# Eight single PSUM banks, a later fetch of x, and seven-product pairs at other places in a decoder layer

## The chip, the core and the metric

The kernel runs on one core of a Trainium2 chip. The metric is the device time of one execution in microseconds (us). The engines are TensorE (PE: matmuls; PEld: its weight loads), VectorE (DVE), ScalarE (ACT), GpSimd (POOL) and SyncE (SP, which here only starts DMAs). Each has its own queue, which it works through in order; semaphores hold an instruction back until what it needs is done. All matmul results land in PSUM, which has eight banks of 512 float32 columns on each of 128 partitions.

## The reference: what is computed

One layer of a decoder on x, 256 tokens by 2048 channels, in float32: a feed-forward half step, a mixer of two kinds of attention, a second feed-forward half step. Each is set between two RMS norms.

```python
for l in range(DEPTH):          # DEPTH = 1
    h = rmsnorm(x, ffn1_pre_g[l])
    x = x + 0.5 * rmsnorm(swiglu_ffn(h, ffn1_w_in[l], ffn1_w_out[l]), ffn1_post_g[l])
    h = rmsnorm(x, mix_pre_g[l])
    y = hybrid_mixer(h, w_in[l], ..., w_branch_sb[l], w_branch_nsa[l], w_out[l])
    x = x + rmsnorm(y, mix_post_g[l])
    h = rmsnorm(x, ffn2_pre_g[l])
    x = x + 0.5 * rmsnorm(swiglu_ffn(h, ffn2_w_in[l], ffn2_w_out[l]), ffn2_post_g[l])

def swiglu_ffn(h, w_in, w_out):
    gate, up = jnp.split(h @ w_in, 2, axis=-1)      # w_in 2048 x 11264
    return (jax.nn.silu(gate) * up) @ w_out         # w_out 5632 x 2048
```

The mixer projects h to queries, keys, values and gates, runs eight heads of stick-breaking attention and eight heads of native sparse attention (compressed, selected and window keys), projects both branches, merges them by gates and projects once more (w_out, 2048 x 2048).

## The kernel before

**Numbers in two parts.** Every float32 factor is written as hi + lo, two values of a shorter format that PE multiplies at full rate, and a product is three matmuls: hi by hi, lo by hi, hi by lo. For a weight, ACT writes hi (`cast`, L1106) into the ring whi, and DVE writes lo = w - hi (`low`, L1109) into wlo. PE's own matmuls all stand in one line, L1322.

**Steps, units, pairs, items.** The layer is a sequence of steps, each a product of the 256 rows with up to 1024 columns of a weight matrix. A step's destination is two banks for the upper 128 rows (h = 0) and two for the lower (h = 1). A *unit* is 128 rows of weights (one kt) by 1024 columns; for one half h it is an *item* of six matmuls, 2 banks by 3 terms. A *pair* is two neighbouring units, 1 MB, and comes by one DMA. In the two feed-forward networks some pairs are computed as a 2x2 block product with seven products in place of eight: three items of 9, 6 and 6 matmuls for four of 6, so 21 matmuls for 24. Such a pair needs sums and differences of weight blocks (DVE, L1189 and L1175) and of the left factors (`side_sums`, L361). Four of its products go to the destination, and P1, P5, P6, P7 are summed over all such pairs of the step in the four *shared* banks, those that the step's destination doesn't use and the next step will. After the last such pair, `combine` (L377) makes of them, with one operation on ACT (L379) and three on DVE (L380, L382, L383), the four blocks that have to be added to the destination, in tmp.

**A feed-forward network** (`ffn`, L392) has 11 in-steps of eight pairs (seven-product pairs 3 and 5, from the second in-step on) and two halves of the way out, j = 0 and j = 1, 22 pairs each, with seven-product pairs at 2, 5, 8, 11, 14. When an in-step's half h is complete, `done` adds tmp to both banks at once (DVE, L406, 1024 columns), ACT makes Silu of the gate (L407), DVE multiplies by the other half (L416) and transposes (L418), ACT copies into `big` (L429), from where it becomes the left factor of the way out. In the halves of the way out `add_shared` (L443, DVE, L445) adds tmp to both banks.

**PSUM.** Four tiles of 1024 columns are allocated (`two_banks`), and `bank[i]` is a half of one. The semaphores are placed when the program is built, from what each instruction reads and writes. Banks 0, 1, 4, 5 also serve the attention as F[0] to F[3]: `scores` of the stick-breaking heads writes F[0] (L502, L503), read by ACT (L504, L505), and `turn` writes F[1] (L518), copied by ACT (L519). Mixer steps are evacuated bank 0 by ACT (L753) and bank 1 by DVE (L755). `evac_nsa` transposes with PE into bank 0 and then bank 1 (L272) and splits each into hi (ACT, L253) and lo (DVE, L254).

**The three ends.** The second half of the way out of FFN 1, the last step of the mixer and that of FFN 2 end in `post_norm` (L327), for each h: sum of squares of bank 0 (ACT, L313), gain on bank 0 (DVE, L320), sum of squares of bank 1, a reduce (L331), scale (L143), a power on POOL (L144), gain on bank 1, and the residual x += (L338). Then PE transposes x for the next step's left factors (L272), or the result is stored (L343).

**Weights and x.** Weights land in four places of 1 MB: two of `raw` and the two halves of the tile x, which hold weights while x itself isn't needed. `load_pairs` (L1052) puts a pair's DMA on SP's queue when a place comes free. Around each of the three ends, for each half, `lend` keeps weights out of x[h] from item w - 14 to w + 25, where w is the item of the last unit of that half, and at w - 14 fetches x[h] back from where it was kept (L1083); at w + 25 `spill` stores it (L1092).

**The order** is made when the program is built: items in a fixed sequence; DVE, ACT and POOL work as tasks with an item at which they are due; and a simple clock of estimated durations (`clock`, `task`, `advance`, `force`) decides where in each queue a task stands. In the order of items the h = 1 half runs one unit behind h = 0, in mixer steps and at the ends of the way out up to five.

Of the kernel before, what the change touches and what calls it, by code (L numbers as in the profile page):

```python
# [36 lines left out]
OUT_DMA = ()  # L37
OUT_SEVEN = (2, 5, 8, 11, 14)
SEVENS = 2
# [57 lines left out]
def layer(ctx: ExitStack, tc: tile.TileContext, a: dict):  # L97
# [24 lines left out]
    st = pool.tile([P, 96], F32, name="st")  # L122
    two_banks = [psum.tile([P, 1024], F32, name=f"bank{i}") for i in range(4)]
    bank = [two_banks[i // 2][:, 512 * (i % 2) : 512 * (i % 2) + 512] for i in range(8)]

# [250 lines left out]

    def combine(p5, p7, p1, p6, p57):  # L377

        nc.scalar.copy(tmp[:, 0, 0:512], p1)  # L379
        nc.vector.tensor_add(u2, p6, tmp[:, 0, 0:512])  # L380
        mid = tmp.rearrange("p h c -> p (h c)")[:, 512:1536].rearrange("p (b c) -> p b c", b=2)
        nc.vector.tensor_add(mid, p57.rearrange("p (b c) -> p b c", b=2), u2.unsqueeze(1).to_broadcast([P, 2, 512]))  # L382
        nc.vector.tensor_add(tmp[:, 1, 512:1024], p7, tmp[:, 0, 512:1024])  # L383
        spend("ACT", 512)
        clock["DVE"] = max(clock["DVE"], clock["ACT"])
        spend("DVE", 512, 1024, 512)

    def both(banks):

        return two_banks[next(i for i in range(4) if bank[2 * i] is banks[0])]  # L390

    def ffn(win, wout, factor, norm_next, flip, out=None):  # L392
        ins = []
        for n in range(NF):
            def dest(h, n=n):
                b = 4 * h + 2 * ((n + flip) % 2)
                return bank[b : b + 2]
# [3 lines left out]
            def done(h, n=n, dest=dest, seven=seven):  # L401
# [3 lines left out]
                if seven:  # L405
                    nc.vector.tensor_add(tmp[:, h, :], both(dest(h)), tmp[:, h, :])  # L406
                    nc.scalar.activation(s, s, AF.Silu, scale=rs(h))  # L407
                    spend("DVE", 1024)
                    spend("ACT", 512)
                    u = d  # L410
                else:
                    nc.scalar.activation(s, g, AF.Silu, scale=rs(h))
                    spend("ACT", 512)
# [29 lines left out]
        def add_shared(h, dest):  # L443
            y = both(dest(h))
            nc.vector.tensor_add(y, y, tmp[:, h, :])  # L445
            spend("DVE", 1024)

        outs = []
        for j in range(2):
# [14 lines left out]

            slot7 = lambda i, j=j: (j * len(OUT_SEVEN) + OUT_SEVEN.index(i)) % SEVENS
            s = step(wout, 22 * j, KF, lhs, dest, done, segs=SWAP, seven=OUT_SEVEN, by_dma=OUT_DMA, combine=combine, slot7=slot7)
            s["j"] = j
# [628 lines left out]
    for h in range(2):  # L1096
        lend(h, a["x"][h * P : (h + 1) * P, :], 10 + 6 * h, 20 + 6 * h)
        for n, s in enumerate(big_ends):
            w = where["u", h, s["last"]]
            last_ = n == len(big_ends) - 1  # L1100
            lend(h, a["x"][h * P : (h + 1) * P, :] if n == 0 else kept(h), w - 14, len(items) if last_ else w + 25)
            if not last_:
                at(w + 25, lambda h=h: spill(h))
# [157 lines left out]
    def matmuls(kind, sub, q):  # L1261
# [20 lines left out]
        rb, ra, rt = q["at"]  # L1282
        p5, p7, p1, p6 = shared(s)[:4]
        todo = (
# [9 lines left out]
    def shared(s):  # L1294
        mine = [b.name if hasattr(b, "name") else id(b) for h in range(2) for b in s["dest"](h)]
        idx = [k for k in range(8) if not any(bank[k] is c for h in range(2) for c in s["dest"](h))]
        assert len(idx) == 4
        return [bank[k] for k in idx] + [both([bank[idx[0]]])]

# [94 lines left out]
    for nf, (ins, outs) in enumerate(ffns):  # L1394
# [13 lines left out]
        for i in IN_SEVEN:  # L1408
            held[IN_SEVEN.index(i)] = last_use(ins[-1], [2 * i], 0)
        for s in outs:  # L1410
            for i in OUT_SEVEN:
                slot = s["slot7"](i)
# [113 lines left out]
```

## Time and profile before

| | us |
|---|---|
| three timed runs: median (lowest to highest) | 2125.14 (2124.61 to 2126.95) |
| the profiled execution: its own time | 2127.88 |
| the profiled execution: span, first to last instruction | 2126.1 |
| DVE busy in the span | 1482.6 |
| ACT busy in the span | 1264.3 |

Views of the profile used here: the busy table of the page; the waits (who waited for whom, in us, how often, the longest); groups of one line with what its engine waited for before it; the timeline (start in us from the span's start, duration, engine, line, operation, names out<-in, count, and in brackets the idle time of that engine before it and what ended it); and sums over windows (for each stretch its length, the busy time of each engine with the count of instructions, the granted TensorE clock, DMA share, GB/s). PE's matmuls are pipelined: each shows about 0.39 us but they start 0.227 us apart, so times are best read from start to start.

### The profile page before, as it was taken

The page shows a single profiled execution, that of the slowest core. Times are in us where ns is not written, and L with a number is a line of the kernel's source. Part 1 is how long each engine was busy: PE and PEld are TensorE (multiplying, and loading weights), DVE is VectorE, ACT ScalarE, POOL GpSimd, SP SyncE. Part 2 cuts the span into 40 slices and gives each one's busy share as a digit, 9 for nine tenths or more (in the row PEclk, how much of TensorE's full clock was granted, in tenths as well). Part 3 has the DMA queues.
Part 4 walks back from the last instruction along what each step waited for, and adds up shares of the span by engine and source line. Part 5 has one row for each costly group of instructions (what it writes and reads, how often), then busy time and mean ns, then how long its engine had stood idle before and what let it go on. Part 6 is the DMA issues. An engine that isn't in the chain of part 4 may idle for free.

```text
span 2126.1 us, 24260 instructions
## 1 busy us (share of the span) xinstructions
PE 2083.1 (98%) x9422; PEld 1718.1 (81%) x9422; DVE 1482.6 (70%) x1582; ACT 1264.3 (59%) x1603; POOL 113.4 (5%) x139
## 2 busy tenths in 40 slices
PE   8999999999999999999999999999999999999998
PEld 7788888887788787779888887878888888878886
DVE  5877777787777678653555456566777777887685
ACT  6766666667766453442545443446766666776672
POOL 0000000001111000000000000000000000011110
PEclk9999999999999999999999999999999999999999
DMA  8756766667977474445434454557766675678884
GB/s 314 269 207 230 236 221 217 226 225 217 287 224 228 173 260 178 178 160 181 159 138 160 178 198 161 205 193 260 249 220 217 230 239 205 222 217 259 248 233 168
DMA packets 77875, 456.45 MB, mean 215 GB/s; under 512 B 9152, under 2 KB 10048, under 8 KB 28608
## 3 DMA queue, kind: packets, MB, share of 16 engines
q1 hardware_dynamic: 59760, 407.57, 52.1%
q0 software_dynamic: 17712, 47.19, 11.7%
q8 instruction: 74, 1.21, 0.2%
q14 instruction: 41, 0.34, 0.0%
q10 hardware_dynamic: 288, 0.14, 0.0%
HBM read 427.61 MB, written 6.29 MB: 204 GB/s over the span
## 4 chain that ended last, share of the span: by engine, by line
PE 83%; DVE 8%; ACT 4%; DMA 3%; issue 2%; POOL 0%; ACTq 0%; DVEq 0%; POOLq 0%
PE bank L1322 79%; DVE wlo L1109 4%; ACT whi L1106 2%; DMA raw<-in_wm_dram 1%; DVE big L281 1%; ACT big L429 1%; DMA x<-in_wf1o_dram 1%; PE bank L272 1%; PE bank L556 0%; DVE tmp L406 0%; PE bank L702 0%; PE bank L651 0%; DVE x L338 0%; DMA raw<-in_wf2o_dram 0%; DVE tmp L416 0%
## 5 line engine op out<-in xcount | busy, mean ns | idle before, releaser
L1322 PE MATMUL bank<-whi,xhi 128*128 128x512 f32 (+1 forms) x2708 | 860.6, 391 | 9.6 <-ACT whi L1106 7.6
L1322 PE MATMUL bank<-wlo,xhi 128*128 128x512 f32 (+1 forms) x2708 | 854.1, 389 | 5.1 <-DVE wlo L1109 5.0
L1322 PE MATMUL bank<-whi,xlo 128*128 128x512 f32 (+1 forms) x2708 | 851.5, 388 | 0.0
L1109 DVE TENSOR_TENSOR wlo<-raw,whi 128x1024 fp32r<-128x1024 f32 (+4 forms) x342 | 506.4, 1498 | 192.1 <-ACT whi L1106 191.0
L1322 PEld LDWEIGHTS bank<-wlo,xhi 128*128 128x128 f32 x2708 | 507.6, 188 | 112.1 <-DVE wlo L1109 8.7
L1322 PEld LDWEIGHTS bank<-whi,xhi 128*128 128x128 f32 x2708 | 503.5, 188 | 112.0 <-ACT whi L1106 9.6
L1322 PEld LDWEIGHTS bank<-whi,xlo 128*128 128x128 f32 x2708 | 507.7, 188 | 104.4
L1109 DVE TENSOR_TENSOR wlo<-x,whi 128x1024 fp32r<-128x1024 f32 (+3 forms) x273 | 429.4, 1591 | 185.9 <-ACT whi L1106 185.3
L1106 ACT ACTIVATE whi<-raw 128x1024 fp32r<-128x1024 f32 (+4 forms) x352 | 448.9, 1294 | 169.5 <-PE bank L1322 98.1
L1106 ACT ACTIVATE whi<-x 128x1024 fp32r<-128x1024 f32 (+3 forms) x281 | 378.5, 1367 | 150.6 <-PE bank L1322 105.4
L429 ACT COPY big<-tmp 32x256 f32<-32x256 f32 x352 | 142.4, 405 | 34.1 <-DVE tmp L418 30.0
L407 ACT ACTIVATE tmp<-tmp,st 128x512 f32<-128x512 f32 x40 | 29.1, 726 | 112.8 <-DVE tmp L406 112.8
L266 POOL DMA_DIRECT2D xlo<-big x80 | 70.0, 875 | 434.2 <-ACT xlo L265 421.5
L1322 PE MATMUL bank<-wlo,ahi 128*128 128x512 f32 x240 | 84.3, 392 | 4.5 <-DVE wlo L1109 4.4
L1322 PE MATMUL bank<-whi,ahi 128*128 128x512 f32 x240 | 83.9, 390 | 0.6 <-ACT whi L1106 0.6
L1322 PE MATMUL bank<-whi,alo 128*128 128x512 f32 x240 | 83.9, 390 | 0.0
L379 ACT COPY tmp<-bank 128x512 f32<-128x512 f32 x24 | 14.1, 588 | 93.6 <-PE bank L1322 93.6
L265 ACT ACTIVATE xlo<-big 128x512 fp32r<-128x512 f32 x80 | 49.6, 621 | 15.6 <-PE bank L1322 15.5
L406 DVE TENSOR_TENSOR tmp<-bank,tmp 128x1024 f32<-128x1024 f32 x40 | 48.2, 1205 | 13.9 <-PE bank L1322 13.8
L1322 PEld LDWEIGHTS bank<-wlo,ahi 128*128 128x128 f32 x240 | 44.7, 188 | 15.9 <-DVE wlo L1109 7.0
L1322 PEld LDWEIGHTS bank<-whi,ahi 128*128 128x128 f32 x240 | 45.0, 188 | 10.7 <-ACT whi L1106 1.4
L416 DVE SCALAR_TENSOR_TENSOR tmp<-tmp,st 128x512 f32<-128x512 f32 x40 | 30.1, 751 | 33.0 <-ACT tmp L407 33.0
(169 smaller groups left out, 1058.9 us busy)
## 6 DMA issues: line engine op xcount, KB each, us to landing
raw<-in_wf2i_dram SPq DMA_DIRECT2D x49, 1024.0 KB, 6.3
raw<-in_wf1i_dram SPq DMA_DIRECT2D x45, 1024.0 KB, 6.3
raw<-in_wm_dram SPq DMA_DIRECT2D x41, 1024.0 KB, 4.8
x<-in_wf1i_dram SPq DMA_DIRECT2D x40, 1024.0 KB, 6.0
x<-in_wf2i_dram SPq DMA_DIRECT2D x39, 1024.0 KB, 5.9
x<-in_wm_dram SPq DMA_DIRECT2D x31, 1024.0 KB, 4.8
raw<-in_wf2o_dram SPq DMA_DIRECT2D x24, 1024.0 KB, 7.4
raw<-in_wf1o_dram SPq DMA_DIRECT2D x22, 1024.0 KB, 6.4
```

The costliest lines, as they stand in the source:

```text
L265: t = task("ACT", 0.62, lambda: nc.scalar.activation(lo, src, AF.Copy, scale=-1.0), rel=rel, due=due)
L266: d = task("POOL", 0.86, lambda: nc.gpsimd.dma_start(lo, src, accum_op=ALU.add), deps=[t], rel=rel, due=due)
L272: nc.tensor.transpose(dst[:, i * P : (i + 1) * P], src[:, i * P : (i + 1) * P], ident)
L281: vector.transpose(dst[32 * q : 32 * q + 32, :, rows], v[:, :, q, :])
L379: nc.scalar.copy(tmp[:, 0, 0:512], p1)
L406: nc.vector.tensor_add(tmp[:, h, :], both(dest(h)), tmp[:, h, :])
L407: nc.scalar.activation(s, s, AF.Silu, scale=rs(h))
L416: nc.vector.scalar_tensor_tensor(d, u, rs(h), s, ALU.mult, ALU.mult)
L429: nc.scalar.copy(o[32 * q : 32 * q + 32, :, :, rows], v[:, :, :, q, :])
L1106: nc.scalar.activation(hi, src, AF.Copy)
L1109: nc.vector.tensor_sub(lo, src, hi.bitcast(F32))
L1322: nc.tensor.matmul(b[:, 0:n], left, w[:, o : o + n], start=(i, k) in firsts, stop=(i, k) in lasts, skip_group_check=id(items[i][2]["step"] ...
```

## The change

1. The four tiles of 1024 columns become eight tiles of 512, one per bank. Whatever worked on two banks in one operation is split in two: `done` of the in-steps (L406), `add_shared` (L445), and the middle operation of `combine` (L382). The function `both` goes.
2. The shared products take their four banks in the order P1, P5, P6, P7 (before: P5, P7, P1, P6).
3. The seven-product pairs of the way out are given for each half: pairs 3, 6, 9, 12, 15, 18 for j = 0 and 2, 5, 8, 11, 14 as before for j = 1. The two slots of the left factors' sums alternate over the eleven.
4. x's halves are fetched back at item w - 6 for w - 14; until then weights may use them.

```diff
-OUT_SEVEN = (2, 5, 8, 11, 14)
+OUT_SEVEN = ((3, 6, 9, 12, 15, 18), (2, 5, 8, 11, 14))
...
-    two_banks = [psum.tile([P, 1024], F32, name=f"bank{i}") for i in range(4)]
-    bank = [two_banks[i // 2][:, 512 * (i % 2) : 512 * (i % 2) + 512] for i in range(8)]
+    bank = [psum.tile([P, 512], F32, name=f"bank{i}") for i in range(8)]
...
-    def combine(p5, p7, p1, p6, p57):
+    def combine(p1, p5, p6, p7):
 
         nc.scalar.copy(tmp[:, 0, 0:512], p1)
         nc.vector.tensor_add(u2, p6, tmp[:, 0, 0:512])
-        mid = tmp.rearrange("p h c -> p (h c)")[:, 512:1536].rearrange("p (b c) -> p b c", b=2)
-        nc.vector.tensor_add(mid, p57.rearrange("p (b c) -> p b c", b=2), u2.unsqueeze(1).to_broadcast([P, 2, 512]))
+        nc.vector.tensor_add(tmp[:, 0, 512:1024], p5, u2)
+        nc.vector.tensor_add(tmp[:, 1, 0:512], p7, u2)
         nc.vector.tensor_add(tmp[:, 1, 512:1024], p7, tmp[:, 0, 512:1024])
...
                 if seven:
-                    nc.vector.tensor_add(tmp[:, h, :], both(dest(h)), tmp[:, h, :])
+                    nc.vector.tensor_add(s, g, s)
+                    nc.vector.tensor_add(d, u, d)
                     nc.scalar.activation(s, s, AF.Silu, scale=rs(h))
...
         def add_shared(h, dest):
-            y = both(dest(h))
-            nc.vector.tensor_add(y, y, tmp[:, h, :])
-            spend("DVE", 1024)
+            for b in range(2):
+                y = dest(h)[b]
+                nc.vector.tensor_add(y, y, tmp[:, h, b * 512 : (b + 1) * 512])
+            spend("DVE", 512, 512)
...
-            slot7 = lambda i, j=j: (j * len(OUT_SEVEN) + OUT_SEVEN.index(i)) % SEVENS
+            slot7 = lambda i, j=j: (j * len(OUT_SEVEN[0]) + OUT_SEVEN[j].index(i)) % SEVENS
...
-            lend(h, a["x"][h * P : (h + 1) * P, :] if n == 0 else kept(h), w - 14, len(items) if last_ else w + 25)
+            lend(h, a["x"][h * P : (h + 1) * P, :] if n == 0 else kept(h), w - 6, len(items) if last_ else w + 25)
```

More of the change, by code (lines that the diff above doesn't have):

```diff
@@ L385, in combine @@
         clock["DVE"] = max(clock["DVE"], clock["ACT"])
-        spend("DVE", 512, 1024, 512)
-    def both(banks):
-        return two_banks[next(i for i in range(4) if bank[2 * i] is banks[0])]
+        spend("DVE", 512, 512, 512, 512)
     def ffn(win, wout, factor, norm_next, flip, out=None):
@@ L443, in add_shared @@
         def add_shared(h, dest):
-            y = both(dest(h))
-            nc.vector.tensor_add(y, y, tmp[:, h, :])
-            spend("DVE", 1024)
+            for b in range(2):
+                y = dest(h)[b]
+                nc.vector.tensor_add(y, y, tmp[:, h, b * 512 : (b + 1) * 512])
+            spend("DVE", 512, 512)
         outs = []
@@ L463, in done @@
                     post_norm(h, dest(h), factor, norm_next, out)
-            slot7 = lambda i, j=j: (j * len(OUT_SEVEN) + OUT_SEVEN.index(i)) % SEVENS
-            s = step(wout, 22 * j, KF, lhs, dest, done, segs=SWAP, seven=OUT_SEVEN, by_dma=OUT_DMA, combine=combine, slot7=slot7)
+            slot7 = lambda i, j=j: (j * len(OUT_SEVEN[0]) + OUT_SEVEN[j].index(i)) % SEVENS
+            s = step(wout, 22 * j, KF, lhs, dest, done, segs=SWAP, seven=OUT_SEVEN[j], by_dma=OUT_DMA, combine=combine, slot7=slot7)
             s["j"] = j
@@ L1282, in matmuls @@
         rb, ra, rt = q["at"]
-        p5, p7, p1, p6 = shared(s)[:4]
+        p1, p5, p6, p7 = shared(s)
         todo = (
@@ L1297, in shared @@
         assert len(idx) == 4
-        return [bank[k] for k in idx] + [both([bank[idx[0]]])]
+        return [bank[k] for k in idx]
     program = [matmuls(*i) for i in items]
@@ L1409, in layer @@
             held[IN_SEVEN.index(i)] = last_use(ins[-1], [2 * i], 0)
-        for s in outs:
-            for i in OUT_SEVEN:
+        for j, s in enumerate(outs):
+            for i in OUT_SEVEN[j]:
                 slot = s["slot7"](i)
```

## The prediction

> **What bounds the kernel now.** I read the busy table, the waits of TensorE, and then single stretches of it. The busy table says that PE is never long without work:
>
> ```profile
> span 2126.1 us, 24260 instructions
> ## 1 busy us (share of the span) xinstructions
> PE 2083.1 (98%) x9422; PEld 1718.1 (81%) x9422; DVE 1482.6 (70%) x1582; ACT 1264.3 (59%) x1603; POOL 113.4 (5%) x139
> ```
>
> The profiled execution took 2127.88 us around this span, 2.74 above the median of the three timed runs (2125.14). With PE full, time can go in three ways only: fewer matmuls, less idle time of PE, a shorter tail behind PE. The waits of PE name the idle time (line; whom it waits for; us, times, longest):
>
> ```profile
> PE bank L1322 <- DVE wlo L1109: 9.4, 10, 1.7
> PE bank L1322 <- ACT whi L1106: 8.2, 3, 7.6
> PE bank L272 <- DVE x L338: 6.9, 4, 3.7
> PE bank L502 <- ACT att L519: 4.3, 7, 0.6
> PE bank L272 <- DVE xlo L254: 1.8, 2, 0.9
> PE bank L1322 <- DVE big L755: 1.7, 3, 1.0
> PE bank L272 <- ACT big L526: 0.5, 1, 0.5
> ```
>
> The 7.6 is the start of the kernel, which the change leaves alone. The price of a matmul comes from the last in-step of FFN 1 (first row below, matmuls of L1322 alone): two pairs with seven products and six plain ones are 2x21 + 6x24 = 186 matmuls in 42.16 us, 0.2267 us each. PE does not idle there.
>
> ```profile
> 434.63:476.79 42.16, 42.16 (x187) 34.92 (x186) 1.00 0.62 214
> 476.79:597.77 120.98, 117.32 (x514) 95.97 (x513) 1.00 0.84 251
> 1878.57:2000.13 121.56, 119.08 (x514) 97.13 (x513) 0.99 0.82 242
> ```
>
> Rows two and three are the first half of the way out (j = 0) of FFN 1 and 2: 17 plain and 5 seven-product pairs, 513 matmuls, 116.28 us at that price. They take 120.98 and 121.56, so 4.7 and 5.3 us are lost there.
>
> **Part 1, one more seven-product pair in each j = 0.** Three matmuls fewer, twice: 6 x 0.2267 = **1.4 us**. This is as good as certain, and below what a measurement of this kernel can tell from no change (about 0.2%, 4.3 us).
>
> **Part 2, the first seven-product pair of j = 0 moves from pair 2 to pair 3.** Where the 4.7 us go, as PE and then DVE show it:
>
> ```profile
> 490.31 0.50 PE L1322 MATMUL bank<-whi,ahi 128*128 128x512 f32 x1 [0.29 <-ACT whi L1106]
> 490.64 0.40 PE L1322 MATMUL bank<-whi,xhi 128*128 128x512 f32 x1
> 492.76 0.50 PE L1322 MATMUL bank<-wlo,ahi 128*128 128x512 f32 x1 [1.72 <-DVE wlo L1109]
> ```
> ```profile
> 489.28 2.28 DVE L1109 TENSOR_TENSOR wlo<-x,whi 128x2048 fp32r<-128x2048 f32 x1
> 491.49 1.22 DVE L1109 TENSOR_TENSOR wlo<-raw,whi 128x1024 fp32r<-128x1024 f32 x1
> ```
>
> ```profile
> 474.92 1.75 DVE L1109 TENSOR_TENSOR wlo<-raw,whi 128x1536 fp32r<-128x1536 f32 x1
> ```
>
> The last piece of pair 2 (1.22 us, at 491.49) stands in the DVE queue behind the low half of plain pair 3 (2.28 us), and PE waits 0.29 + 1.72 us; from start to start it is 2.3 (the matmul after a wait starts a little late). A seven-product pair needs of DVE the low half of 1536 columns (1.75, last row), three operations of 1024 (1.22 each) and two of 512 (0.69, L320 below), 6.8 us; a plain one needs 2.28, and just here DVE also evacuates the last in-step. With the seven at pair 3 DVE has 24 x 0.2267 = 5.4 us more until the piece is due, against a deficit of 2.3, so I take this stall as gone in both FFNs. In FFN 2 it costs more:
>
> ```profile
> 1894.70 0.50 PE L1322 MATMUL bank<-wlo,ahi 128*128 128x512 f32 x1 [1.72 <-DVE wlo L1109]
> ```
> ```profile
> 714.08:717.49 3.41, 3.41 (x11) 2.83 (x11) 2.05 (x4) 1.58 (x2) 0.00 (x0) 0.50 0.00 0
> 1895.09:1898.50 3.41, 3.41 (x10) 2.64 (x9) 3.31 (x6) 3.33 (x9) 0.00 (x0) 0.50 0.88 360
> ```
>
> Right behind the stall the granted clock is 0.50 for 3.41 us (second row; the third figure from the end is the granted clock), so about half of it is lost, 1.6 us. The first row is the other such stretch, in part 4. Sum: 2.3 + 2.3 + 1.6 = **6.2 us**; the ends are 8.6 (the two later stalls of j = 0, below, go too) and -2 (the stall moves along with the seven and one more comes). The later stalls I leave as they are, since the sevens keep their distance of three pairs:
>
> ```profile
> 534.13 0.74 PE L1322 MATMUL bank<-wlo,xhi 128*128 128x512 f32 x2 [1.65 <-DVE wlo L1109]
> ```
>
> The Trainium skill, "TensorE: Matmul & The Clock Gate", Part 1, says that the clock is halved after an idle window of about 3.4 us, and that this window runs free of the kernel. The 3.41 us length agrees; the idle window does not, since 1.72 us of waiting was enough at 1894.7, while the same wait at 492.8 cost no clock. By the page's rule this stretch would not hang on the stall, and the sum would be 1.6 us smaller: 2107, inside the forecast's own spread.
>
> **Part 3, eight single banks.** The four rows of L502, L254, L755 and L526 have one thing in common: PE waits for an engine that reads the *other* bank of the same 1024-column tile. L502 writes F[0] = bank 0; L519 reads F[1] = bank 1. They share nothing else: L502 reads q_sb and k_sb, L519 writes att. ACT's own readers of F[0] (L504, L505) stand a head earlier in its queue. The same between ACT and DVE:
>
> ```profile
>   DVE bank L445: 15.3, 2
>   DVE big L320: 11.4, 12
> ```
> ```profile
>   ACT tmp L753: 15.1, 5
> ```
>
> The first fence is what L313 (square of a bank, ACT) waited for: 12 times for L320, the gain on the bank before. The second is L755 (evacuation of bank 1 on DVE) waiting for L753 (bank 0 on ACT). So the four tiles are guarded as wholes, and eight tiles end these waits. L502 gives 4.3, L526 0.5, L254 1.8; of L755's 1.7 I take 1.4, since the first matmul still waits until bank 0 is emptied. **8.0 us**, ends 0 (the guard is something else) and 8.3. These waits lie in the mixer's attention and branch steps; the time is kept if weights go on arriving, which part 6 prices. The Trainium skill, "PSUM — Partial Sum Buffer", section "PSUM bank collisions raise a hardware error", asks for a guard per bank and finds that different banks run clean, while ACT and DVE on one bank must take turns. By this rule the waits across banks are none of the chip's and part 3 is 8.0; if the chip needed them it would be 0, rival B. No run here shows a collision.
>
> **Part 4, the three ends that leave x** (FFN 1, mixer, FFN 2). The tail, ACT's rows and then DVE's:
>
> ```profile
> 2116.62 0.60 ACT L313 ACTIVATE tmp<-bank 128x512 f32<-128x512 f32 x1 [3.40 <-PE bank L1322]
> 2117.11 0.19 ACT L313 ACTIVATION_READ_ACCUMULATOR tmp<-bank 128x1 f32 x1
> 2118.06 0.60 ACT L313 ACTIVATE tmp<-bank 128x512 f32<-128x512 f32 x1 [0.76 <-DVE big L320]
> ```
> ```profile
> 2118.78 0.16 DVE L331 TENSOR_REDUCE st<-st 128x1 f32<-128x4 f32 x1 [0.75 <-ACT tmp L313]
> ```
>
> The square of bank 0 starts when all matmuls are done (2116.62), though the last six write bank 1 only; the square of bank 1 waits for the gain on bank 0. With single banks the first square (its gain still behind it) runs 6 x 0.2267 = 1.4 us earlier, under those matmuls, and the second starts at 2116.62 instead of 2118.06. Everything behind it, reduce, power, residual, store, moves up: **1.4 us** off the end of the kernel. The same chain ends the four waits of L272 for L338 (6.9 us in all, longest 3.7). The three short ones, 6.9 - 3.7 = 3.2 us, are each no longer than 1.4 us: **3.1 us**. The long one, at FFN 1, h = 0, as ACT and DVE show it:
>
> ```profile
> 706.38 1.06 ACT L1106 ACTIVATE whi<-raw 128x1024 fp32r<-128x1024 f32 x1 [5.57 <-DMA raw<-in_wm_dram]
> ```
> ```profile
> 707.48 1.23 DVE L1109 TENSOR_TENSOR wlo<-raw,whi 128x1024 fp32r<-128x1024 f32 x1 [4.92 <-ACT whi L1106]
> 708.62 1.23 DVE L445 TENSOR_TENSOR bank<-bank,tmp 128x1024 f32<-128x1024 f32 x1
> 710.60 0.69 DVE L320 TENSOR_TENSOR big<-bank,gbuf 128x512 f32<-128x512 f32 x1 [0.75 <-ACT tmp L313]
> 712.05 0.16 DVE L331 TENSOR_REDUCE st<-st 128x1 f32<-128x4 f32 x1 [0.75 <-ACT tmp L313]
> ```
>
> L445 stands in DVE behind a weight whose DMA was late. Even if that stays, adding the first bank alone (0.69 for 1.23) and squaring without L320 in between save 0.54 + 0.72 = 1.3 us. If the weight is no longer late (part 5), the add can start when bank 0 is whole, three matmuls into the last item:
>
> ```profile
> 705.89 0.39 PE L1322 MATMUL bank<-whi,xhi 128*128 128x512 f32 x1
> ```
>
> That is 706.8 at the earliest, 1.8 us before 708.62. I take 1.3 of it, so 2.6 in all, ends 1.3 and 3.7. With 1.1 us of wait left, the half clock at 714.08 goes: 1.6. Sum of part 4: 1.4 + 3.1 + 2.6 + 1.6 = **8.7 us**.
>
> **Part 5, x fetched at w - 6 for w - 14.** An item is six matmuls, 1.36 us; the two halves of x serve as weight places 8 x 1.36 = 10.9 us longer, so two more weight pairs go through them and the two raw places are free for the mixer's first weights earlier. That is the late DMA above. The price is x itself. Its fetch takes, over the eight of them,
>
> ```profile
> DMA to landing us min/median/max: 6.9/7.1/10.9
> ```
>
> ```profile
> 713.08 1.41 DVE L338 SCALAR_TENSOR_TENSOR x<-big,st,x 128x512 f32<-128x512 f32 x2
> ```
>
> Item w (h = 0, FFN 1) starts at 705.9, so w - 6 is at 697.7. SP issues in order, so the fetch also stands behind any weight load asked for earlier whose place is not free yet; the fetches and all loads after them wait there, and the residual waits for the fetch. 697.7 + 7.1 = 704.8; behind a load that is some 5 us late, about 710. The residual needs x at 713.08 - 2.6 = 710.5. So it is free, or a little late. I count nothing, ends -4 and +2.
>
> **Part 6, what the split adds.** L406 (10 in-steps, 2 halves, 2 FFNs), L382 (12 steps, 2 FFNs) and L445 (4 per FFN) become two operations each: 40 + 24 + 8 = 72 more on DVE, each 2 x 0.69 - 1.23 = 0.15 us more work (L320 and L445 above), 11 us in all. In the in-steps this is covered: PE loses nothing there, and DVE gains more than it pays, since Silu starts after the first half:
>
> ```profile
>   ACT tmp L407: 33.0, 40
> ```
>
> That is 0.8 us of DVE waiting for Silu, 40 times; the second add now runs under Silu. The shared products also change places among their four banks (P1 first, whose copy on ACT frees it first); no row shows PE waiting for these banks after combine, so that costs nothing either way. I count zero; without that cover, all 11 us would stand in DVE's queue before the weights, and at most the share that falls into the stretches where PE already waits for L1109 would reach PE. PE running ahead meets the next supplier, DVE's L1109, for which it waits 9.4 us in 10 places now. I take **-2** for new waits there, ends -6 and +2.
>
> **Sum.** 1.4 + 6.2 + 8.0 + 8.7 + 0 - 2 = 22.3 us off the profiled 2127.9, so 2105.6. Taken off the median it would be 2102.8, but the profiled run may hold half-clock stretches (3.2 us here) that the others lack, so part of the sum may be missing there. I forecast **2105 us**.
>
> **Rivals.**
> *A, the stall moves with the seven.* DVE is still behind later in j = 0 now (PE's 1.65 us wait at 534.13), so pair 3 or 6 may stall as pair 2 does. Then part 2 gives nothing: 22.3 - 6.2 = 16.1, 2111.
> *B, the banks are not what is guarded.* The waits of L502, L254, L755 stay, and part 4 keeps only the late weight (1.3 + 1.6). Sum 1.4 + 6.2 + 2.9 - 2 = 8.5: 2119 from the profiled time, 2117 from the median. Against it: 12 of 12 gains and squares alternate, without any data in common.
> *C, slower: DVE becomes the bound of j = 0.* One more seven (6.8 - 2.3 = 4.5 us of DVE, besides the sums of its left factors) and the split operations come on top. If DVE falls behind by as much at each seven as it does now at the first, 12 sevens cost 2.3 us each, 27.6, where 4.6 is paid now: 23 more, and say three more half-clock stretches of 1.6. 2127.9 - 16.1 + 23 + 4.8 = 2140; it decides from 16 us of such stalls. Against it: of the five sevens in j = 0 only the first stalls today, and the rest of the loss there is 4.7 - 2.3 = 2.4 us.
> *D, no change.* The stall moves, x is late by 4 us, DVE owes 6, and the long wait stays with its half clock: 1.4 + 0 + 8.0 + 4.5 - 4 - 6 = 3.9, 2124.
>
> **How the numbers follow.** Forecast 0.58, A 0.20, B 0.09, C 0.04, D 0.09. The range reaches over A and B, 2098 (all bounds of parts 2 to 4 good, seen from the median) to 2117. Faster by over 0.2% is the forecast, A and B: 0.87; within 0.2% is D: 0.09; slower is C: 0.04.
>
> **What would show it.** L502 without its wait for L519; L313 no longer waiting for L320; the last square right behind the last matmul and the end 1.4 us nearer to the last matmul; j = 0 at 510 matmuls in 116 to 118 us; no 0.50 in the clock at these two places; the mixer's first weights requested before 700. I am wrong if L1109 takes over as the wait of PE, in j = 0 or in the mixer, with more than the 9.4 us it has now.

## The result, and the profile after

The changed kernel takes **2091.13 us** (median of four runs, 2090.63 to 2092.18) where the kernel before took 2124.88 in the runs beside it (2123.8 to 2126.95). The ratio is 0.9841, with a 95% interval of 0.9824 to 0.9858. The forecast was 2105 us with a range of 2098 to 2117: the direction was right, and the gain, some 34 us, was larger than the best of its ends.

The busy table of the changed kernel, as that of before (busy us, share of the span, count of instructions):

```profile
span 2090.4 us, 24353 instructions
PE 2069.4 (99%) x9416; PEld 1716.4 (82%) x9416; DVE 1497.9 (72%) x1674; ACT 1270.8 (61%) x1609; POOL 113.2 (5%) x139
```

The six matmuls are gone (9422 to 9416), DVE has 92 instructions and 15.3 us of work more, and the span is 35.7 us shorter. PE's busy time fell by only 13.7. The waits of PE, all that the view lists for the changed kernel (who waits for whom; us, times, longest):

```profile
PE bank L1319 <- ACT whi L1103: 7.5, 1, 7.5
PE bank L271 <- DVE x L337: 2.8, 1, 2.8
PE bank L1319 <- DVE wlo L1106: 2.3, 5, 0.7
```

(Line numbers moved by three at most: L1319 is the matmul, L1106 the low half, L1103 the cast, L442 `add_shared`, L312 the square, L319 the gain, L337 the residual, L499 the scores.) All waits for another bank of the same tile are gone: scores for att, the transposes for xlo and big, the matmul for big. PE's waits for the low half fell from 9.4 us in 10 places to 2.3 in 5, where the prediction expected new ones.

Where the time went is read from the first matmul of a step to the first of a later one. The windows of four such stretches, matmuls of L1319 alone (length, busy PE and PEld, granted clock, DMA share, GB/s): the second in-step of FFN 1, its j = 0, five steps of the mixer from the projection of the sparse heads' queries on, in which the attention runs, and j = 0 of FFN 2:

```profile
52.76:94.92 42.16, 42.16 (x187) 34.92 (x186) 1.00 0.70 244
474.36:590.35 115.99, 115.90 (x512) 95.67 (x510) 1.00 0.87 249
840.51:1104.62 264.11, 228.56 (x961) 169.91 (x960) 1.00 0.47 166
1849.80:1965.87 116.07, 115.89 (x511) 95.67 (x510) 1.00 0.86 248
```

The first and third stretch of before (its j = 0 stands in the prediction):

```profile
52.81:97.35 44.54, 43.03 (x187) 34.68 (x186) 1.00 0.70 242
852.97:1127.65 274.68, 229.91 (x961) 169.59 (x960) 1.00 0.45 160
```

All that moved, in us of the two profiled executions (spans 2126.1 and 2090.4), set against the prediction's parts:

| stretch | before | after | gained | part | forecast |
|---|---|---|---|---|---|
| second in-step of FFN 1 | 44.54 | 42.16 | 2.4 | none (chance, below) | 0 |
| j = 0 of FFN 1 and FFN 2 | 242.55 | 232.06 | 10.5 | 1 and 2 | 7.6 |
| mixer's attention | 274.68 | 264.12 | 10.6 | 3 | |
| four later steps of the mixer, with waits for the evacuation | | | 3.4 | 3 | |
| part 3 together | | | 14.0 | 3 | 8.0 |
| j = 1 of FFN 1 and the mixer's first step | 165.07 | 161.22 | 3.9 | 4 | |
| other ends that leave x | | | 2.9 | 4 | |
| tail | 9.92 | 8.48 | 1.4 | 4 | |
| part 4 together | | | 8.2 | 4 | 8.7 |
| two steps of the mixer's projections | 90.13 | 88.94 | 1.2 | none | 0 |
| second in-step of FFN 2 (42.16 in e8, 43.41 in a2) | 42.21 | 42.78 | -0.6 | 6, or chance | -2 |
| sum | | | 35.7 | | 22.3 |

### The profile page after: what moved, and what is told of

The parts are those of the page before. It is cut to its first block, busy times and chain, and to the rows that moved or that the text cites. A ratio compares the mean times of both kernels' runs of the same rounds, so it can differ in the third digit from the quotient of the medians.

```text
span 2090.4 us, 24353 instructions
## 1 busy us (share of the span) xinstructions
PE 2069.4 (99%) x9416; PEld 1716.4 (82%) x9416; DVE 1497.9 (72%) x1674; ACT 1270.8 (61%) x1609; POOL 113.2 (5%) x139
## 3 DMA queue, kind: packets, MB, share of 16 engines
q0 software_dynamic: 17712, 47.19, 11.6%
## 4 chain that ended last, share of the span: by engine, by line
PE 89%; DVE 4%; DMA 3%; ACT 2%; issue 1%; ACTq 0%; DVEq 0%; POOLq 0%; POOL 0%
PE bank L1319 86%; DVE wlo L1106 2%; DVE big L280 2%; DMA raw<-in_wm_dram 1%; ACT whi L1103 1%; PE bank L271 1%; PE bank L553 0%; PE bank L699 0%; DMA raw<-in_wf2i_dram 0%; PE bank L648 0%; DMA raw<-in_wf2o_dram 0%; DMA x<-in_wf1o_dram 0%; DMA x<-in_wf2i_dram 0%; PE bank L693 0%; DMA big<-in_xt_dram 0%
## 5 line engine op out<-in xcount | busy, mean ns | idle before, releaser
L1319 PE MATMUL bank<-whi,xhi 128*128 128x512 f32 (+1 forms) x2698 | 855.9, 390 | 7.6 <-ACT whi L1103 7.5
L1319 PE MATMUL bank<-wlo,xhi 128*128 128x512 f32 (+1 forms) x2698 | 849.7, 388 | 2.1 <-DVE wlo L1106 2.0
L1319 PE MATMUL bank<-whi,xlo 128*128 128x512 f32 (+1 forms) x2698 | 847.3, 388 | 0.0
L1106 DVE TENSOR_TENSOR wlo<-raw,whi 128x1024 fp32r<-128x1024 f32 (+4 forms) x337 | 498.5, 1495 | 209.4 <-ACT whi L1103 208.4
L1319 PEld LDWEIGHTS bank<-wlo,xhi 128*128 128x128 f32 x2698 | 505.3, 188 | 107.5 <-DVE wlo L1106 4.5
L1319 PEld LDWEIGHTS bank<-whi,xlo 128*128 128x128 f32 x2698 | 505.2, 188 | 103.5
L1319 PEld LDWEIGHTS bank<-whi,xhi 128*128 128x128 f32 x2698 | 501.7, 188 | 106.2 <-ACT whi L1103 7.5
L1106 DVE TENSOR_TENSOR wlo<-x,whi 128x1024 fp32r<-128x1024 f32 (+3 forms) x282 | 441.1, 1583 | 185.4 <-ACT whi L1103 184.7
L1103 ACT ACTIVATE whi<-raw 128x1024 fp32r<-128x1024 f32 (+4 forms) x347 | 442.3, 1292 | 205.8 <-PE bank L1319 125.3
L1103 ACT ACTIVATE whi<-x 128x1024 fp32r<-128x1024 f32 (+3 forms) x290 | 388.9, 1360 | 175.9 <-PE bank L1319 114.1
L1319 PE MATMUL bank<-wlo,ahi 128*128 128x512 f32 x248 | 86.5, 389 | 0.3 <-DVE wlo L1106 0.3
L1319 PE MATMUL bank<-whi,ahi 128*128 128x512 f32 x248 | 86.4, 389 | 0.0
L1319 PE MATMUL bank<-whi,alo 128*128 128x512 f32 x248 | 86.4, 389 | 0.0
L1319 PEld LDWEIGHTS bank<-wlo,ahi 128*128 128x128 f32 x248 | 46.5, 188 | 10.3 <-DVE wlo L1106 0.7
L1319 PEld LDWEIGHTS bank<-whi,ahi 128*128 128x128 f32 x248 | 46.6, 188 | 9.7
L1319 PEld LDWEIGHTS bank<-whi,alo 128*128 128x128 f32 x248 | 46.6, 188 | 9.7
L267 ACT ACTIVATE xhi<-big 128x512 fp32r<-128x512 f32 x80 | 49.3, 616 | 0.0
L1172 DVE TENSOR_TENSOR raw<-raw 128x512 f32<-128x512 f32 x66 | 45.7, 692 | 2.2
```

Of the source, the lines that this page charges most:

```text
L267: task("ACT", 0.62, lambda: nc.scalar.activation(hi, src, AF.Copy), rel=rel, due=due)
L1103: nc.scalar.activation(hi, src, AF.Copy)
L1106: nc.vector.tensor_sub(lo, src, hi.bitcast(F32))
L1172: nc.vector.tensor_sub(*b)
L1319: nc.tensor.matmul(b[:, 0:n], left, w[:, o : o + n], start=(i, k) in firsts, stop=(i, k) in lasts, skip_group_check=id(items[i][2]["step"] ...
```

## The experiments

Two theories stood against each other at first. **Tiles** (T in the expectations): the semaphores guard a tile of two banks as a whole, and the single banks bring most of the gain. **Split** (R1): the operations that were cut in two bring it, since DVE's results are ready earlier. Beside them, the new places of the sevens and the later fetch of x had to be priced. Each time is a median, and each ratio is to the kernel before, run beside it (2125.61, 2126.2 and 2125.77 us for the three groups of runs, which were on different chips).

| run | what it is | us | ratio, 95% interval |
|---|---|---|---|
| e1 | the change without new sevens and late x | 2097.14 | 0.9864 [0.985, 0.9879] |
| e2 | e1 with the old tiles of two banks | 2119.00 | 0.9972 [0.9963, 0.9982] |
| e3 | before, with the new sevens | 2118.82 | 0.9967 [0.9953, 0.9981] |
| e4 | before, with the late x | 2126.45 | 1.0002 [0.9993, 1.0012] |
| e5 | the change, with x fetched early | 2093.11 | 0.9847 [0.9832, 0.9862] |
| e6 | the change, with the old sevens | 2095.61 | 0.986 [0.9845, 0.9874] |
| e7 | before, with L406 split | 2118.23 | 0.9965 [0.9952, 0.9977] |
| e8 | the change, with a later weight task | 2090.66 | 0.9836 [0.9822, 0.9851] |
| e9 | e8 with a sixth seven in j = 1 | 2090.14 | 0.9834 [0.982, 0.9849] |
| e10 | e2 with two of eight banks single | 2107.92 | 0.9922 [0.9905, 0.9938] |
| e11 | e8 with x fetched early | 2090.69 | 0.9836 [0.9822, 0.9851] |
| a2 | the change once more | 2094.05 | 0.9854 [0.984, 0.9869] |

**e1 and e2: tiles or split operations.** Both have the split operations and the new order of the shared products, the old sevens and x at w - 14; they differ in the tiles alone. On PE, DVE, ACT and POOL the two have the same instructions in the same order.

```diff
-OUT_SEVEN = ((3, 6, 9, 12, 15, 18), (2, 5, 8, 11, 14))
+OUT_SEVEN = ((2, 5, 8, 11, 14), (2, 5, 8, 11, 14))
...
-            lend(h, a["x"][h * P : (h + 1) * P, :] if n == 0 else kept(h), w - 6, len(items) if last_ else w + 25)
+            lend(h, a["x"][h * P : (h + 1) * P, :] if n == 0 else kept(h), w - 14, len(items) if last_ else w + 25)
```

e2 takes this in addition:

```diff
-    bank = [psum.tile([P, 512], F32, name=f"bank{i}") for i in range(8)]
+    two_banks = [psum.tile([P, 1024], F32, name=f"bank{i}") for i in range(4)]
+    bank = [two_banks[i // 2][:, 512 * (i % 2) : 512 * (i % 2) + 512] for i in range(8)]
```

> Of the change only the eight single banks with the split operations and the new order of the shared products; sevens at 2, 5, 8, 11, 14 in both halves, x fetched at w - 14. Theory T (a PSUM tile is guarded as a whole, so PE, ACT and DVE wait across its two banks; each such wait costs more than its idle time in the waits view): 2101 to 2107 us; L502 without waits, L313 without waits for L320, the tail 1.4 us shorter, the heads' period 8.5 us for 9.4, and the stall at the first seven of j = 0 still there. Rival R1 (not the guard but the shorter operations help): the same time here, but see the next run. Rival R2 (the later fetch of x brought what came on top of the forecast): 2110 or more.

> Before, with the operations split in two and the new order of the shared products as in the change, but on the four tiles of two banks. T: 2122 to 2128 us, the waits of L502 for L519 (4.3 us) and of L313 for L320 (12 times) as before. R1: 2101 to 2107, like the single banks.

The tiles are worth 2119.00 - 2097.14 = 21.9 us, about what parts 3 and 4 gained above (14.0 + 8.2 = 22.2). The waits of e2's PE and, from the group of its square L313, what ACT waited for:

```profile
PE bank L500 <- ACT att L517: 4.3, 7, 0.6
PE bank L272 <- DVE xlo L254: 1.8, 2, 0.9
PE bank L1320 <- DVE big L753: 1.6, 3, 1.0
```
```profile
  DVE big L320: 11.4, 12
```

They are those of before to 0.1 us, though every operation on two banks is gone. So the waits come from the tile, and rival B is out. Both runs came out lower than expected, and one place shows a part of it, j = 0 of FFN 1 in e2, whose sevens stand where they stood before:

```profile
477.16:594.87 117.71, 116.88 (x515) 96.16 (x513) 1.00 0.87 258
```

It took 120.98 before. The split theory was wrong of the waits and right of something else: a part of the operations that were cut in two ends a stall that part 2 of the prediction gave to the sevens alone.

**e7: the add of the in-steps alone.** Before, with this edit:

```diff
-                    nc.vector.tensor_add(tmp[:, h, :], both(dest(h)), tmp[:, h, :])
+                    nc.vector.tensor_add(s, g, s)
+                    nc.vector.tensor_add(d, u, d)
                     nc.scalar.activation(s, s, AF.Silu, scale=rs(h))
-                    spend("DVE", 1024)
+                    spend("DVE", 512, 512)
```

> Before, with only the add of the in-steps' ends (L406) split in two, on the four tiles of two banks. If the stall at the first seven of j = 0 hangs on that add (Silu may start after its first half): j = 0 at 117 to 118.5 us in both FFNs for 121.0 and 121.6, 2118 to 2121 us in all. If it was the order of the shared products or combine's split: j = 0 at 120 or more, 2123 to 2127.

The two j = 0 fall to 117.76 and 117.63 us and the whole to 2118.23: this edit is worth 8 us. The last in-step of FFN 1, the timeline of DVE in the kernel before and then in e7, and from the group of e7's multiplication what DVE waited for:

```profile
476.59 1.22 DVE L406 TENSOR_TENSOR tmp<-bank,tmp 128x1024 f32<-128x1024 f32 x1
478.66 0.75 DVE L416 SCALAR_TENSOR_TENSOR tmp<-tmp,st 128x512 f32<-128x512 f32 x1 [0.85 <-ACT tmp L407]
...
482.06 0.75 DVE L416 SCALAR_TENSOR_TENSOR tmp<-tmp,st 128x512 f32<-128x512 f32 x1 [0.79 <-ACT tmp L407]
```
```profile
476.10 0.69 DVE L406 TENSOR_TENSOR tmp<-bank,tmp 128x512 f32<-128x512 f32 x1 [0.53 <-PE bank L1323]
476.71 0.68 DVE L407 TENSOR_TENSOR tmp<-bank,tmp 128x512 f32<-128x512 f32 x1
477.58 0.75 DVE L417 SCALAR_TENSOR_TENSOR tmp<-tmp,st 128x512 f32<-128x512 f32 x1 [0.19 <-ACT tmp L408]
...
480.45 0.75 DVE L417 SCALAR_TENSOR_TENSOR tmp<-tmp,st 128x512 f32<-128x512 f32 x1 [0.19 <-ACT tmp L408]
```
```profile
  ACT tmp L408: 7.8, 40
```

From the start of the add to the multiplication DVE needs 478.66 - 476.59 = 2.07 us before and 1.48 in e7, 0.6 less, since Silu runs under the second add. Over all in-steps DVE's wait for Silu falls from 33.0 to 7.8 us. In the in-steps themselves PE does not wait and nothing is gained. But the evacuation of the last one stands in DVE's queue ahead of the low halves for j = 0, where PE did wait. The second multiplication comes 482.06 - 476.79 = 5.27 us after the first matmul of j = 0 before, and 480.45 - 477.26 = 3.19 after it in e7: 2.1 us earlier, where PE's two waits at pair 2 were 2.0. Silu under the second add gives about 1.2 of this, 0.6 for each half. The edit does one thing more: it gives the simple clock two operations of 512 columns in place of one of 1024, and 25 other instructions of DVE's queue and 33 of ACT's then stand at another place, some of them here. How the 8 us are shared between the earlier Silu and the new order was not tried.

**e3: the sevens alone.** Before, with the new places:

```diff
-OUT_SEVEN = (2, 5, 8, 11, 14)
+OUT_SEVEN = ((3, 6, 9, 12, 15, 18), (2, 5, 8, 11, 14))
```

> Before, with only the new places of the sevens (3, 6, 9, 12, 15, 18 in j = 0). If the place alone ends the stall: both halves j = 0 at 116 to 117 us for 121.0 and 121.6, no 0.50 in the clock there, 2114 to 2117 us. Rival A (the stall moves with the seven, and it was the banks that ended it): j = 0 at 119 to 121 us, 2120 to 2124.

```profile
474.56:591.88 117.32, 116.19 (x511) 95.56 (x510) 1.00 0.87 251
1873.23:1990.44 117.21, 116.21 (x512) 95.56 (x510) 1.00 0.85 251
```

The halves j = 0 gain 242.55 - 234.53 = 8.0 us (forecast of parts 1 and 2: 7.6). The stall at the first seven is gone, and pair 3 has none. But a shorter one comes at pair 6, in FFN 1 and likewise in FFN 2 (0.88 us), 1.2 us each from start to start:

```profile
508.73 0.73 PE L1322 MATMUL bank<-wlo,ahi 128*128 128x512 f32 x2 [0.92 <-DVE wlo L1109]
```

The later wait, at a plain pair, falls from 1.65 and 0.47 us to 0.22 and 0.12, which is worth 1.8 us. The whole gains 6.8, less than the 8.6 to 11.6 that were expected. In its profiled execution the clock was at 0.50 for 6.83 us from 707.33, where before it was so for 3.41 us from 714.08; how much of that the timed runs hold is not known.

**e6: how much of the sevens is left beside the split.** The change, with the sevens of e1.

> The changed kernel with the sevens of j = 0 at 2, 5, 8, 11, 14 again. The halves j = 0 at 117.3 to 117.6 us as with the banks alone, for 116.0 and 116.1; 2094 to 2097 us. If place and banks added up as the forecast has it, the stall at the first seven (2.3 us each) would be back: j = 0 at 118.5 or more and 2098 or more.

2095.61 lies in what was expected, but its interval overlaps with that of the change run again (a2), so the stretch must be asked. Its two j = 0 take 117.32 and 117.52 us. That is 234.84, and 232.06 in the change: beside the split the sevens give 2.8 us, of which 1.4 are the six matmuls. Alone each edit takes most of the same loss. At 0.2267 us each, 2 x 513 matmuls need 232.6 us; before lost 10.0 over that. e7 loses 2.8 (7.2 taken away), e3 loses 234.53 - 231.2 = 3.3 (6.6 away), and the change, which has both and the single banks, 0.9 (9.1 away, not 13.8).

**e4, e5 and e11: the fetch of x.** e4 is the kernel before with w - 6 for w - 14, e5 the change with w - 14:

```diff
-            lend(h, a["x"][h * P : (h + 1) * P, :] if n == 0 else kept(h), w - 6, len(items) if last_ else w + 25)
+            lend(h, a["x"][h * P : (h + 1) * P, :] if n == 0 else kept(h), w - 14, len(items) if last_ else w + 25)
```

> Before, with only x fetched at w - 6. T: 2122 to 2127 us, the weight that PE's long wait at the end of FFN 1 hangs on is asked for no earlier against PE than before (5.6 us ahead of item w). R2: 2115 or less, with that weight asked for 10 us earlier.

> The changed kernel with x fetched at w - 14 again. If the later fetch brings nothing by itself: 2090 to 2093 us, no stage apart by more than 1 us. If it matters once PE waits less elsewhere: 2095 or more, with the loss at the ends that leave x.

Neither can be told from its counterpart: 2126.45 against 2125.61, and 2093.11, which lies between the two medians of the change (2091.13 and 2094.05). The queue of SP at the end of FFN 1, before and after (start and the time that the issues span; the first fetch of x is that of h = 0, the second that of h = 1):

```profile
683.09 0.42 SPq L1083 DMA_DIRECT2D x<-in_x_dram  x1
...
689.38 0.42 SPq L1083 DMA_DIRECT2D x<-in_x_dram  x1
691.48 0.33 SPq L1063 DMA_DIRECT2D raw<-in_wm_dram  x1
700.32 0.33 SPq L1063 DMA_DIRECT2D raw<-in_wm_dram  x1
```
```profile
679.83 0.33 SPq L1060 DMA_DIRECT2D raw<-in_wm_dram  x1
680.21 0.42 SPq L1080 DMA_DIRECT2D x<-in_x_dram  x1
692.73 2.60 SPq L1060 DMA_DIRECT2D raw<-in_wm_dram  x2
695.38 0.42 SPq L1080 DMA_DIRECT2D x<-in_x_dram  x1
```

Item w of h = 0 starts at 705.89 before and 698.47 after (shown under e8); in this paragraph its start is w, in us. The two halves of x are fetched at w - 22.8 and w - 16.5 before, at w - 18.3 and w - 3.1 after, so 4.5 and 13.4 us later. The first of the mixer's weights is asked for at w - 18.6 after and w - 14.4 before. But the second, the one that was late, goes out at w - 5.7 after and w - 5.6 before: the later fetch of x didn't bring it forward. In e4 it is w - 5.6 as well. What holds it can be read, though no run tried it: after the fetch of x SP waits 12.0 us for DVE's low half, which empties a raw place. These low halves stand in DVE's queue behind an add of the shared products, before which DVE itself waits 8.34 us for PE:

```profile
690.28 1.30 DVE L442 TENSOR_TENSOR bank<-bank,tmp 128x512 f32<-128x512 f32 x2 [8.34 <-PE bank L1319]
691.49 3.48 DVE L1106 TENSOR_TENSOR wlo<-raw,whi 128x1024 fp32r<-128x1024 f32 x3
```

The first of the three ends at about 691.49 + 1.23 = 692.72, and the load goes out at 692.73.

**e8: what the late weight still costs.** The change, with the earliest item at which the mixer's first weights are prepared moved from 12 to 8 items ahead of their use:

```diff
-            first = start - (AHEAD if not b or u > b + 6 else 12 if u < b + 3 else 4)
+            first = start - (AHEAD if not b or u > b + 6 else 8 if u < b + 3 else 4)
```

> The changed kernel with one number more: the first three units of a bound step may be prepared 8 items ahead for 12, which puts the low half of the mixer's third unit behind add_shared, the gains and the residual in the DVE queue at the end of FFN 1 (and one unit likewise at the end of the mixer). If PE's long wait (2.8 us) hangs on that late weight: about 1 us of it left, 2088 to 2090 us. If the chain from the last matmul to the residual is the bound by itself: the wait stays over 2.3 us, 2091.

The end of FFN 1 (h = 0) after the change: PE at the start of item w, ACT, DVE, and PE behind the wait:

```profile
698.47 0.39 PE L1319 MATMUL bank<-whi,xhi 128*128 128x512 f32 x1
...
705.54 0.66 PE L271 MATMUL bank<-cst,x 128*128 128x128 f32 x4 [2.83 <-DVE x L337]
```
```profile
699.43 1.06 ACT L1103 ACTIVATE whi<-raw 128x1024 fp32r<-128x1024 f32 x1 [7.87 <-DMA raw<-in_wm_dram]
```
```profile
700.53 1.23 DVE L1106 TENSOR_TENSOR wlo<-raw,whi 128x1024 fp32r<-128x1024 f32 x1 [5.56 <-ACT whi L1103]
701.67 1.29 DVE L442 TENSOR_TENSOR bank<-bank,tmp 128x512 f32<-128x512 f32 x2
...
704.74 1.42 DVE L337 SCALAR_TENSOR_TENSOR x<-big,st,x 128x512 f32<-128x512 f32 x2
```

The adds still stand behind the low half of the late weight. In e8 they don't, as its DVE and its PE show:

```profile
700.85 1.38 DVE L442 TENSOR_TENSOR bank<-bank,tmp 128x512 f32<-128x512 f32 x2 [4.37 <-PE bank L1319]
...
705.34 1.22 DVE L1106 TENSOR_TENSOR wlo<-raw,whi 128x1024 fp32r<-128x1024 f32 x1
```
```profile
704.81 0.44 PE L271 MATMUL bank<-cst,x 128*128 128x128 f32 x2 [0.60 <-DVE x L337]
```

The wait falls from 2.83 to 0.60 us, and the stretch of j = 1 and the mixer's first step from 161.22 to 159.07. Part of this is the execution: the same wait is 1.44 us in e5 and 3.20 in a2. What it follows is the cast of the late weight, which starts when the weight has landed:

| execution | start of item w | cast of the late weight | cast after w | PE's long wait | wait less cast |
|---|---|---|---|---|---|
| e5 | 699.64 | 699.20 | -0.44 | 1.44 | 1.88 |
| e6 | 700.50 | 700.37 | -0.13 | 1.74 | 1.87 |
| e1 | 700.86 | 701.33 | 0.47 | 2.33 | 1.86 |
| the change | 698.47 | 699.43 | 0.96 | 2.83 | 1.87 |
| a2 | 701.50 | 702.82 | 1.32 | 3.20 | 1.88 |
| before | 705.89 | 706.38 | 0.49 | 3.75 | 3.26 |
| e4 | 703.47 | 704.11 | 0.64 | 3.90 | 3.26 |

With single banks the wait is 1.87 us longer than the cast is late, on the tiles of before 3.26 (3.25 in e3 and e7, 3.45 in e2). So the banks take 1.4 us off this wait whatever the weight does, and the rest hangs on the weight. In e8, e9 and e11, where the adds no longer stand behind it, the wait is 0.60, 0.61 and 0.61. The whole of e8, 2090.66, cannot be told from the change.

**e10: is the gain of a wait the idle time that the view names?** e2 with two of the eight banks single, so that the scores (bank 0) and att's turn (bank 1) no longer share a tile (instructions and their order are those of e2):

```diff
-    two_banks = [psum.tile([P, 1024], F32, name=f"bank{i}") for i in range(4)]
-    bank = [two_banks[i // 2][:, 512 * (i % 2) : 512 * (i % 2) + 512] for i in range(8)]
+    bank = [psum.tile([P, 512], F32, name=f"bank{i}") for i in range(2)]
+    two_banks = [psum.tile([P, 1024], F32, name=f"pair{i}") for i in range(3)]
+    bank += [two_banks[i // 2][:, 512 * (i % 2) : 512 * (i % 2) + 512] for i in range(6)]
```

> The split operations with old sevens and x at w - 14 (as in the run with split operations alone, 2119 us), but banks 0 and 1, the attention's F[0] and F[1], as single tiles and the other six as three tiles of two. The waits of L502 for L519 must go, those of L254 and of L526 (other banks) stay. If a removed wait is worth its idle time: the steps qnsa, kv1, kv2 together 4.3 to 5 us shorter than with split operations alone. If it costs more, by the late start of the next matmuls: 6.5 to 8 us shorter; 2108 to 2113 in all, since the ends of h = 0 in banks 0 and 1 gain too.

The mixer's attention in e2 and then in e10:

```profile
849.27:1123.77 274.50, 229.75 (x962) 169.61 (x960) 1.00 0.46 160
```
```profile
844.45:1112.74 268.29, 229.70 (x961) 169.59 (x960) 1.00 0.47 164
```

In this stretch only the seven waits of the scores are gone, 4.3 us of idle time. It is 6.2 us shorter, 0.89 per wait where the view says 0.61: each of these waits costs 0.83 to 0.89 from start to start, for 0.57 to 0.62 us of idle time.

**e9 and e11: a better version?** e9 is e8 with six sevens in j = 1 also; e11 is e8 with x at w - 14.

```diff
-OUT_SEVEN = ((3, 6, 9, 12, 15, 18), (2, 5, 8, 11, 14))
+OUT_SEVEN = ((3, 6, 9, 12, 15, 18), (2, 5, 8, 11, 14, 17))
```

> The kernel with the weight behind add_shared (8 items ahead for 12) and a sixth seven in j = 1, at pair 17: three matmuls fewer in each FFN, 1.4 us. If no new wait comes: 2087 to 2089 us. If DVE falls behind late in j = 1: 2091 or more, with PE's waits for wlo there.

> The changed kernel with the weight behind add_shared and x fetched at w - 14: 2089 to 2091 us if the later fetch brings nothing; over 2092 if it does.

e9 missed its 2087 to 2089, and e11 is where it was expected. Their medians and e8's lie 0.4 to 1.0 us below the change's best one, and all intervals overlap: no version is shown to beat the change.

**a2: the same kernel again.** No edit.

> The changed kernel again, on the same chip as the three below: 2090 to 2093 us. The second in-step of FFN 1 takes 44.5 or 42.2 us by chance of the start, if the 2.4 us that separate the two profiles there are none of the change's.

Its profiled execution took 2098.62 us, 6.4 more than the first one. Windows of a2: the second in-step of FFN 1, and then, for all engines, 6.83 us at the end of FFN 1 (the third figure from the end is the clock). They begin 1.97 us into the long wait of 3.20 us, which ends at 708.94:

```profile
53.20:97.95 44.75, 43.04 (x187) 34.68 (x186) 1.00 0.70 241
```
```profile
707.71:714.54 6.83, 5.60 (x15) 4.56 (x16) 4.37 (x6) 1.58 (x2) 0.39 (x1) 0.50 0.00 0
```

The second in-step has the 44.75 us of the kernel before (44.54), without any edit. So the 2.4 us there are no gain of the change.

## Why the prediction was off

The direction held, and so did the mechanisms of parts 1 to 4, but for the late weight of part 4; the sum was 13.4 us short of the profiled difference. Part 3 makes 6.0 of this, j = 0 makes 2.9, the start of FFN 1 2.4 by chance, part 6 1.4, two steps of the mixer's projections 1.2, and part 4 takes 0.5 back.

**Part 1** held: 1.4 us, as the count of matmuls shows.

**Part 2** held for the stall at pair 2: the new place ended it. That e3 gave 8.0 us with part 1, against 7.6, is in part luck. **Rival A** came by half there: the sevens at pair 6 cost 1.2 us each, and the later wait, which the part left as it was, gave 1.8 back. In the change itself no wait of j = 0 is over 0.2 us, and rival A did not come. The 1.6 us for the half clock were luck too: in e4 the same wait of 1.72 us at the same matmul has the clock at 1.00 behind it (last section).

**Part 3 failed in its size; its mechanism held.** That the tile is what is guarded is shown by e2 against e1. The step that failed is "L502 gives 4.3, L526 0.5, L254 1.8; of L755's 1.7 I take 1.4": it took the idle time of the waits for the time that they cost. The scores behind a turn in the changed kernel; the wait of before is shown first:

```profile
872.21 0.49 PE L518 MATMUL bank<-cst,att 128*128 128x128 f32 x3
873.26 0.49 PE L502 MATMUL bank<-big 128*128 128x128 f32 x2 [0.57 <-ACT att L519]
873.59 0.60 PE L503 MATMUL bank<-big 128*128 128x256 f32 x2
873.83 0.58 PE L1322 MATMUL bank<-whi,xhi 128*128 128x512 f32 x1
```
```profile
859.74 0.49 PE L515 MATMUL bank<-cst,att 128*128 128x128 f32 x3
860.06 0.39 PE L499 MATMUL bank<-big 128*128 128x128 f32 x2
860.28 0.60 PE L500 MATMUL bank<-big 128*128 128x256 f32 x2
860.53 0.82 PE L1319 MATMUL bank<-whi,xhi 128*128 128x512 f32 x2
```

From the turn to the next matmul of L1322 it was 1.62 us and is 0.79: 0.83 lost, of which the view calls 0.57 idle. The rest lies on both sides. Without a wait the scores start 0.32 us after the turn's first matmul, while the modelled end of the turn, from which idle time is counted, is 0.48 us after it (873.26 - 0.57 - 872.21): 0.16. And the matmuls after the wait start 0.33 apart instead of 0.22: 0.11. The prediction itself had read the stall of part 2 from start to start (2.3 for 0.29 + 1.72), and did not do so here. The other waits are of the same kind. Set matmul by matmul beside the change, the kernel before loses time in 15 places of the attention, the seven of the scores 6.2 us for 4.3 us of idle time and eight others 4.2 for 2.6, and in six places of the four later steps, 3.3 us for 1.9. That is 13.7 us for 8.8 us idle, about 0.2 more at each place. Five of the 21 show 0.04 us of idle time or less and still cost 0.24 to 0.28 each. Of the 6.0 us that the part fell short some 4.9 are this price, and 0.8 is idle time that it left out (0.3 of L755, and two more waits of 0.5 in all).

**Part 4** gave 8.2 against 8.7, with another make-up. The tail is exactly as forecast; its last square, on ACT:

```profile
2082.35 0.60 ACT L312 ACTIVATE tmp<-bank 128x512 f32<-128x512 f32 x1 [0.67 <-PE bank L1319]
```

No gain stands between the two squares any more. The short waits are gone. The long one was to lose 2.6 of 3.7 us and lost 0.9. From the low half to the residual DVE now takes 704.74 - 700.53 = 4.21 us where it took 713.08 - 707.48 = 5.60, so the 1.3 for the split and the square came (1.39). The other 1.3, for a weight "no longer late", did not; the low half even starts 2.06 us after the start of w instead of 1.59, and 1.39 - 0.47 = 0.92. The table under e8 shows the same: 1.4 from the banks in every execution, and a weight that lands when it lands. The half clock went in this execution, but a2 shows that it need not.

**Part 5 failed in one claim**, "the two raw places are free for mixer's first weights earlier. That is the late DMA above": the first was asked for earlier, the late one was not (SP's queue in e4 and in the change). Its cost, nothing, was right (e4, e5).

**Part 6 failed in both numbers.** "I count zero" overlooked that the 0.8 us of DVE that it had found, 40 times, counts at the one place where DVE is what PE waits for next: with the new order 8 us alone (e7), and at most 2.5 beside the sevens (the two j = 0 gain 10.5 in the change, which has the single banks too, and 8.0 in e3). And the -2 for new waits on L1109 was -0.6 at most, while that wait fell from 9.4 to 2.3 us. **Rival C**, DVE as the bound of j = 0, rested on the same price with the wrong sign; 116.0 us for 510 matmuls leave it 0.4. **Rival D** needed several of these costs and none came. The low end of the range, 2098, was also 1 us below its own bounds: 2102.8 less 2.4, 0.3 and 1.1 for the good ends of parts 2 to 4 is 2099.0.

## What to carry to other kernels

Price a wait of TensorE from the start of the matmul before it to the start of the second or third after it, against the same place without the wait, and not by the idle time that a view names: here 0.6 us named were 0.8 to 0.9 lost. If several edits end one stall, price what each does alone and take the loss away once. And time saved on an engine with slack is not nothing where that engine's queue runs on into a stage in which it is what the busy engine waits for.

## What the runs showed of the hardware

The half clock is not a function of the wait alone. All six executions with a wait of 3.20 to 3.90 us at the end of FFN 1 had it there. Below that there is no order: none with the change's 2.83, 3.41 us of it with 2.33 (e1), none with 2.05 (e10). In j = 0 of FFN 2, behind the same wait of 1.72 us at the same matmul, before had 3.41 us of it and e4 none (window for all engines):

```profile
1892.88:1896.50 3.62, 3.62 (x16) 3.02 (x17) 3.49 (x6) 3.53 (x9) 0.00 (x0) 1.00 0.88 344
```

The lengths seen in these stages are 3.41 and 6.83, one or two of the same piece. The three of 6.83 (a2, e3, e4) began 2.0 to 2.4 us after PE fell idle, while the wait still ran; those of 3.41 began after the end of the wait, by 0.2 to 1.4 us. The Trainium skill, "TensorE: Matmul & The Clock Gate", Part 1, has a window of 3413 ns that runs free of the kernel; the lengths agree. It also has the clock fall after at least one idle window of about 3.4 us; here it fell after 1.72, and in a2 1.97 us into a wait.

The second in-step of FFN 1 takes 42.16 or 44.75 us in two executions of the changed kernel, with the same instructions in the same order. In the second PE waits there for two low halves, 1.7 us in all; in the first it doesn't. What makes them late was not tried.
